# Second FFN of a decoder layer: plain weight units dealt out among mixed ones, a fifth bank, another way for the last gated tile, operand sums sooner

## The chip, the cores and the metric

The kernel runs on one core of a Trainium2 chip. The metric is the device time of one execution in microseconds; lower is better. Engines: TensorE (PE: matmuls, PEld: its weight loads), VectorE (DVE), ScalarE (ACT), GpSimd (POOL) and SyncE (SP). The last two issue most of the transfers here.

## What is computed

One decoder layer on 16 meta tokens and 256 tokens of width 2048, in float32: a half-step gated FFN, an attention and convolution mixer, and a second half-step gated FFN. The change lies in the second FFN:

```python
def swiglu(x, w_gate, w_up, w_down):
    return (jax.nn.silu(x @ w_gate) * (x @ w_up)) @ w_down
...
        u = rms_norm(h, ffn2_norm_g[l])
        h = h + 0.5 * swiglu(u, ffn2_w_gate[l], ffn2_w_up[l], ffn2_w_down[l])
    return h[:, N_META:]
```

Here `h` has 256 rows that count (two tiles of 128 tokens, j = 1 and 2), the weights are 2048 x 5632 (gate, up) and 5632 x 2048 (down).

## The kernel before

**Precision.** Every float32 operand is split into a rounded part and a remainder (`hi`, `lo`; `whi` and `wlo` for weights). A product is three matmuls: hi x hi, hi x lo and lo x hi (`trio`, L467). ScalarE makes `whi` (L237), VectorE makes `wlo = raw - whi` (L238).

**Stages of the second FFN** (`ffn_tokens`, from L730). Tokens are stationary, 512 weight columns stream. The 5632 hidden columns come in 11 tiles of 512, in two groups of 6 and 5 (`GROUPS`). An *up part* computes gate and up of one tile for both token tiles; its gated product goes to `mid`. After a group's up parts come two *down parts* (d = 0 and 2), each for 1024 output columns, which multiply the group's `mid` by the down weights. So the order is: six up parts, two down parts, five up parts, two down parts.

**Mixed blocks.** The sum over k is cut into *quads*: two k blocks of 128 rows, two token tiles and two column halves, that is eight block products. A *plain* quad does all eight (blocks `c`). A *mixed* quad does seven products `P1` to `P7` of sums and differences of blocks (Strassen's scheme in Winograd's form); the weight sums are made early in the kernel by jobs and lie in device memory (`sums_up`, `sums_down`), the operand sums of tokens are made on chip (`combos`). In an up part quads 0 to 4 of 8 are mixed (not in the first part), in a down part quads 0 to 3 of 12 or 10.

**Units.** A *unit* is two weight blocks, 128 x 1024 in all, split by one `whi` and one `wlo` instruction. A plain unit has four products (12 matmuls), a mixed unit two (6 matmuls). `mixed_first` and `plain_first` (L97, L114) list the units of a part; `parts_of_ffn2` joins them. An up part before is: P1 and P2 of all mixed quads, P6, P7, P5 (15 mixed units with P4 and P3 begun), then P3, P4 and the three plain quads, 24 units. A down part begins with plain units.

**Loads.** `loads_of` joins two units of one kind (`h`: straight from the weights, `m`: made sums) into a load of 1 MB if they lie at most four units apart. A load goes to one of four buffers in turn (three `raw`, one `raws`), on SP's queue, in order; a buffer is free when both units in it are split. ScalarE and VectorE run up to four units ahead of TensorE: `whi` and `wlo` have four buffers.

**Order of side work.** `Stream.next` is called once per unit, at = n: it issues the work that is due *first* (even slots of `put`), then the split of unit n + 3, then the work that is *waiting* (odd slots). A slot s means unit s // 2, counted from the moment of the call. `LAG` holds the slots. All engines run their queues in order.

**After an up part** the banks are gathered (`gather`), `silu` runs on ScalarE, `times` on VectorE. Then the gated tile must be turned (tokens to columns). For all tiles but a group's last: two 32 x 32 block turns (`turn_gated`, L717), then `move_blocks`: one write to device memory (`hold`, L725) and four reads back (L728) on POOL's queue, then `split_blocks` (L911, L912). For a group's last tile: sixteen turns of 32 rows each that need no move (`turn_columns`, L590), then `split_last` (L541, L542). Down parts need the last tile where they come to the highest quads: unit 12 of 30 in group 0's first part, unit 8 of 26 in group 1's.

**Banks.** `banks` deals four single banks and two double ones to the sums of a part. In an up part the last quarter of the output, `c[2, 1]`, shares its bank with P1, P5 and P6; `gather` takes both. `copy` (L866) moves a finished sum from a bank to `u`.

Of the kernel before, what the change touches and what calls it, by code (L numbers as in the profile page):

```python
# [15 lines left out]
P = 128  # L16
# [63 lines left out]
    silu=(1, 1), times=(3,), last_turn=(9, 9, 11, 13), last_split=14, drain=(0, 2, 4), below=7,  # L80
    act_combos=(6, 10, 14, 18, 23), act_split=(9, 13, 17, 21, 25), factors=(7, 10, 12), out=(1, 1, 5, 17),
# [15 lines left out]
def mixed_first(mixed, plain):  # L97

    own = in_twos(of_kind("P1", mixed) + of_kind("P2", mixed))
    made = in_twos(sum((of_kind(x, mixed) for x in ("P6", "P7", "P5", "P4")), []))  # L100
    rest = in_twos(of_kind("P3", mixed) + sum(plain_pairs(plain), []))
    early = -(-3 * len(mixed) // 2)
    seq = [("h", x) for x in own] + [("m", x) for x in made[:early]]
    made = made[early:]
    for i, x in enumerate(rest):
        seq.append(("h", x))
        if i >= 2 and i % 2 == 0 and made:
            seq.append(("m", made.pop(0)))
    assert not made
    return seq  # L110


def plain_first(mixed, plain, lead):

    pairs = plain_pairs(plain)
    seq = [("h", x) for x in pairs[:lead]]
    pairs = pairs[lead:]
    seq += [("h", x) for x in in_twos(of_kind("P1", mixed) + of_kind("P2", mixed))]
    for name in ("P6", "P7", "P5", "P4"):
        seq += [("m", x) for x in in_twos(of_kind(name, mixed))]  # L120
        if name in ("P6", "P7"):
            seq.append(("h", pairs.pop(0)))
    seq += [("h", x) for x in in_twos(of_kind("P3", mixed))]
    return seq + [("h", x) for x in pairs]


def parts_of_ffn2():

    out = []
    for g, n in enumerate(GROUPS):  # L130
        for f in range(n):
            mixed = MIXED if g or f else ()
            plain = [i for i in range(8) if i not in mixed]
            seq = mixed_first(mixed, plain) if mixed else [("h", x) for x in plain_pairs(plain)]
            out.append((("up", g, f), mixed, seq))
        for d in (0, 2):
            m = DOWN_MIXED[g][d // 2]
            mixed = tuple(range(m))
            plain = range(m, 2 * n)
            left = 2 * len(plain)  # L140
            out.append((("down", g, d), mixed, plain_first(mixed, plain, left - 2 if not d else left - 8)))
# [156 lines left out]
def tile_decoder_layer(  # L298
# [74 lines left out]
    act = const.tile([P, KD, 2, PITCH], F32R, name="act")  # L373
# [1369 lines left out]
```

## Time and profile before

| what | value |
|---|---|
| median of 3 runs | 2138.37 us (2136.25 to 2138.52) |
| the profiled execution, its own time | 2135.43 us |
| its span, first to last instruction | 2133.3 us |
| mean granted clock of TensorE | 0.997 |
| VectorE, ScalarE busy | 1584.8 us, 1087.0 us |
| first and last matmul of the second FFN (L470) | 1421.6 us, 2127.5 us |

A row of the groups names line, engine, operation, what it writes and reads, shape and count; after the first bar stand the busy time in us and the mean duration of one in ns, after the second the engine's idle time just before such instructions and what ended it. A row of the timeline has start and duration in us, and in brackets the idle time before it and its releaser. A matmul's shown duration overlaps the next one's; the pace is read from the starts.

### The profile page before, as it was taken

The numbers are of one execution on the slowest core, as the hardware profiler recorded it, in microseconds if no ns is written. First come the engines' busy times: TensorE is split into PE (matmuls) and PEld (weight loads), VectorE is DVE, ScalarE is ACT, GpSimd is POOL, SyncE is SP. The second block draws the span as 40 slices with busy tenths as digits, with TensorE's granted clock in tenths as the row PEclk, the third lists the DMA queues.
The fourth block names the chain that finished last, engine by engine and source line by source line (L and its number), as shares of the span: only waits on it lengthen the run. The fifth ranks groups of instructions, "written<-read, shape, count | busy, mean of one in ns | idle before, by whom it ended". The sixth has DMA issues, their size and how long they took to land.

```text
span 2133.3 us, 31823 instructions
## 1 busy us (share of the span) xinstructions
PE 2111.1 (99%) x12704; PEld 1884.9 (88%) x12704; DVE 1584.8 (74%) x2134; ACT 1087.0 (51%) x1373; POOL 128.7 (6%) x225
## 2 busy tenths in 40 slices
PE   9999999999999999999999999999999999999988
PEld 9999999999999998799988888887777788787767
DVE  7667666676676758877688688768787787787786
ACT  6444433344444445465544444457666566666654
POOL 0000000000000000000000000010000000000000
PEclk9999999999999999999999999999999999999999
DMA  7788888889888868855468886677889677889855
GB/s 265 266 319 314 331 313 325 316 316 332 312 325 318 314 216 300 334 181 176 158 245 327 315 316 227 212 261 243 313 316 327 245 276 261 314 306 327 295 210 213
DMA packets 97669, 601.61 MB, mean 282 GB/s; under 512 B 10480, under 2 KB 11248, under 8 KB 36336
## 3 DMA queue, kind: packets, MB, share of 16 engines
q1 hardware_dynamic: 64800, 445.42, 57.4%
q0 software_dynamic: 32144, 153.10, 19.7%
q8 instruction: 99, 1.62, 0.3%
q10 hardware_dynamic: 576, 1.05, 0.2%
q14 instruction: 50, 0.41, 0.1%
HBM read 521.41 MB, written 78.12 MB: 281 GB/s over the span
## 4 chain that ended last, share of the span: by engine, by line
PE 74%; issue 18%; DMA 4%; DVE 2%; ACT 1%; POOL 1%; DVEq 0%; ACTq 0%; POOLq 0%
PE single L470 5%; PE pd L435 4%; PE pd L437 4%; PE pd L436 4%; PE pg L437 4%; PE pu L437 4%; PE pg L436 4%; PE pu L436 4%; PE pu L435 4%; PE pg L435 4%; PE double L470 3%; DMA hold<-mt 3%; PE pgt L463 3%; PE pgt L465 3%; PE pgt L464 3%
## 5 line engine op out<-in xcount | busy, mean ns | idle before, releaser
L238 DVE TENSOR_TENSOR wlo<-raw,whi 128x1024 fp32r<-128x1024 f32 (+1 forms) x762 | 916.1, 1212 | 470.8 <-ACT whi L237 464.3
L237 ACT ACTIVATE whi<-raw 128x1024 fp32r<-128x1024 f32 (+1 forms) x762 | 792.2, 1049 | 849.3 <-PE pd L436 144.4
L435 PE MATMUL pd<-mid,whi 128*128 128x272 f32 x704 | 201.7, 286 | 0.0
L436 PE MATMUL pd<-mid,whi 128*128 128x272 f32 x704 | 201.7, 286 | 0.0
L437 PE MATMUL pd<-mid,wlo 128*128 128x272 f32 x704 | 201.7, 286 | 0.0
L470 PE MATMUL single<-whi,act 128*128 128x512 f32 x552 | 195.0, 390 | 2.0 <-ACT act L794 1.5
L435 PE MATMUL pu<-act,whi 128*128 128x272 f32 x672 | 192.6, 287 | 0.0
L436 PE MATMUL pu<-act,whi 128*128 128x272 f32 x672 | 192.5, 287 | 0.0
L435 PE MATMUL pg<-act,whi 128*128 128x272 f32 x672 | 192.5, 286 | 0.0
L436 PE MATMUL pg<-act,whi 128*128 128x272 f32 x672 | 192.5, 286 | 0.0
L437 PE MATMUL pg<-act,wlo 128*128 128x272 f32 x672 | 192.5, 286 | 0.0
L437 PE MATMUL pu<-act,wlo 128*128 128x272 f32 x672 | 192.5, 286 | 0.0
L645 DVE TENSOR_TENSOR made<-made 128x512 f32<-128x512 f32 x264 | 180.6, 684 | 2.7 <-DMA made<-in_wj_dram 2.7
L470 PE MATMUL double<-whi,act 128*128 128x512 f32 x504 | 180.4, 390 | 0.0
L238 DVE TENSOR_TENSOR wlo<-raws,whi 128x1024 fp32r<-128x1024 f32 (+1 forms) x91 | 108.6, 1207 | 33.8 <-ACT whi L237 33.0
L435 PEld LDWEIGHTS pd<-mid,whi 128*128 128x128 f32 x704 | 132.6, 188 | 0.0
L436 PEld LDWEIGHTS pd<-mid,whi 128*128 128x128 f32 x704 | 132.6, 188 | 0.0
L437 PEld LDWEIGHTS pd<-mid,wlo 128*128 128x128 f32 x704 | 132.6, 188 | 0.0
L437 PEld LDWEIGHTS pu<-act,wlo 128*128 128x128 f32 x672 | 126.6, 188 | 0.0
L435 PEld LDWEIGHTS pu<-act,whi 128*128 128x128 f32 x672 | 126.6, 188 | 0.0
L436 PEld LDWEIGHTS pg<-act,whi 128*128 128x128 f32 x672 | 126.6, 188 | 0.0
L435 PEld LDWEIGHTS pg<-act,whi 128*128 128x128 f32 x672 | 126.6, 188 | 0.0
(342 smaller groups left out, 4353.5 us busy)
## 6 DMA issues: line engine op xcount, KB each, us to landing
raw<-in_wgu_dram SPq DMA_DIRECT2D x86, 1024.0 KB, 6.0
raw<-in_w_dram SPq DMA_DIRECT2D x83, 1024.0 KB, 6.7
made<-in_wj_dram POOLq DMA_DIRECT2D x66, 1024.0 KB, 9.0
sums_up<-made POOLq DMA_DIRECT2D x50, 1024.0 KB, 5.6
raw<-in_wd_dram SPq DMA_DIRECT2D x44, 1024.0 KB, 6.2
raw<-sums_up SPq DMA_DIRECT2D x37, 1024.0 KB, 7.1
raws<-in_w_dram SPq DMA_DIRECT2D x25, 1024.0 KB, 7.0
raw<-in_wcv_dram SPq DMA_DIRECT2D x24, 1024.0 KB, 4.8
```

Source lines behind the costliest of these rows:

```text
L237: nc.scalar.activation(hi[:, :n], raw, AF.Copy)
L238: nc.vector.tensor_sub(lo[:, :n], raw, hi[:, :n].bitcast(F32))
L435: nc.tensor.matmul(ps, whi, xhi, start=first, stop=False)
L436: nc.tensor.matmul(ps, whi, xlo, start=False, stop=False)
L437: nc.tensor.matmul(ps, wlo, xhi, start=False, stop=last)
L463: nc.tensor.matmul(ps, xhi, whi, start=k + i == 0, stop=False)
L464: nc.tensor.matmul(ps, xhi, wlo, start=False, stop=False)
L465: nc.tensor.matmul(ps, xlo, whi, start=False, stop=k + i == n - 1)
L470: nc.tensor.matmul(ps, x(a), w[b], start=first and i == 0, stop=last and i == 2, skip_group_check=halting)
L645: getattr(nc.vector, f"tensor_{op}")(to, a, b)
```

## The change

1. **Up parts** (`mixed_up` for `mixed_first`): the plain units, which stood at the end, are dealt out one after every two mixed units from unit 8 on. The order of kinds is half of P1 and P2, then P7 and P6, and so on. The 24 units are now: eight mixed; then plain ones at 8, 10, 13, 16, 19 and 23 among the mixed.
2. **Fifth bank**: the last quarter `c[2, 1]` has a bank of its own, apart from the one of P1, P5 and P6; so VectorE adds the copy of P5 to that of P7 (one 128 x 512 addition a part more).
3. **Slots**: the three steps of `gather` come at units 0, 2 and 4 of the next part, the second `silu` a unit later, `times` at unit 5, the turns behind the third and fourth plain unit (13, 16).
4. **A group's last gated tile** takes the same way as the others: two turns, one write to device memory, four reads back. It is turned at units 6 and 7 of the down part, moved from unit 8 on, and rounded at units 14 and 15 (group 0) or 10 and 11 (group 1).
5. **First down parts** (`mixed_down`): the plain units that need that tile come after P1 and P2, at unit 16 (group 0) and unit 12 (group 1).
6. **Operand sums** for the down parts are made at units 2, 4, 6, 8 in place of 7, 9, 11, 13, in the same buffers for both groups. The gated tile gets a buffer of its own; `act` is laid out anew, with no instruction more.
7. The blocks of a weight job stand in another order in memory, with the same four sums.

Matmuls, loads by bytes, and splits are the same in number. Lines of the changed kernel lie 4 to 7 further down.

```diff
 LAG = dict(
-    silu=(1, 1), times=(3,), last_turn=(9, 9, 11, 13), last_split=14, drain=(0, 2, 4), below=7,
+    gather=(0, 2, 4), silu=(1, 3), times=10, drain=(0, 2, 4), below=(2, 4, 6, 8, 10),
...
+    half = -(-len(mixed) // 2)
     own = in_twos(of_kind("P1", mixed) + of_kind("P2", mixed))
...
+    made = in_twos(sum((of_kind(x, mixed) for x in ("P7", "P6", "P5", "P4")), []))
     pairs = plain_pairs(plain)
...
+    seq = [("h", x) for x in own[:half]] + [("m", x) for x in made[:half]]
+    rest = [("h", own[half])] + [("m", x) for x in made[half : len(mixed)]] + [None]
...
+    for x in rest:
+        if len(pairs) > 1 and (run == 2 or x is None):
             seq.append(("h", pairs.pop(0)))
...
+def mixed_down(mixed, first, then, last):
...
+    seq = [("h", x) for x in first + own + then[:-2]]
+    for name, more in (("P7", then[-2:-1]), ("P6", then[-1:]), ("P5", []), ("P4", [])):
+        seq += [("m", x) for x in in_twos(of_kind(name, mixed))] + [("h", x) for x in more]
+    return seq + [("h", x) for x in in_twos(of_kind("P3", mixed)) + last]
...
+            if not d:
+                seq = mixed_down(mixed, range(m, 2 * n - 2), range(2 * n - 2, 2 * n), ())
...
-            def banks(apart):
-                one, two = (i for i in range(4) if i not in busy)
-                m = singles[busy[0]] if apart else singles[two]
+            def banks(at_once):
+                free = [i for i in range(4) if i not in held]
+                one, two, m = (*free, held[0]) if at_once else (free[1], held[0], free[0])
...
+            def middle_of(g, f, box, at, then):
+                to = mid[:, 4 * f : 4 * f + 4]
+                put(turn_gated(box), (2 * at[0] + 1, 2 * at[1] + 1))
+                st.put(lambda: move_blocks(box["x"]), 2 * at[1] + 2)
...
-                        put([lambda r=r: turn(r) for r in range(4)], LAG["last_turn"])
-                        st.put(lambda to=to, box=box, f=f, g=g: split_last(to, box["m"], f, g), LAG["last_split"])
+                        middle_of(g, f, box, (6, 7), (4 * n - 10, 4 * n - 9))
```

Two places in the engines' queues. First SP, the loads of the third up part of group 0; `in_w` are blocks straight from the weights, `sums_up_2` made sums; two rows of one buffer name are two of its turns. Before (units 0 and 1, 2 and 3, 4, 5 and 6, 7 and 8, 9 to 12, 13 and 14, 15 and 17, 16 and 19):

```order
L214 DMA raws<-in_w_dram 128x2048
L214 DMA raw<-in_w_dram 128x2048
L214 DMA raw<-in_w_dram 128x1024
L214 DMA raw<-sums_up_2_75 128x2048
L214 DMA raws<-sums_up_2_75 128x2048
L214 DMA raw<-sums_up_2_75 128x2048 x2
L214 DMA raw<-in_w_dram 128x2048
L214 DMA raws<-in_w_dram 128x2048
L214 DMA raw<-sums_up_2_75 128x2048
```

Now (units 0 and 1, 2 and 6, 3 to 5 and 7, 8 and 10, 9 and 12, 11 and 13, 14 and 15, 16 and 19):

```order
L218 DMA raw<-in_w_dram 128x2048
L218 DMA raws<-in_w_dram 128x2048
L218 DMA raw<-sums_up_2_75 128x2048 x2
L218 DMA raw<-in_w_dram 128x2048
L218 DMA raws<-sums_up_2_75 128x2048
L218 DMA raw<-in_w_dram 128x2048
L218 DMA raw<-sums_up_2_75 128x2048
L218 DMA raw<-in_w_dram 128x2048
```

Weights and made sums alternate, and a load's two units may lie four apart: `raws` holds units 2 and 6, and its next load, for units 9 and 12, stands behind unit 6's split.

Second VectorE, in the first down part of group 1, around the turns of the last gated tile (`few` held it before, `gated` holds it now; `few` alone is the operand sums). Before:

```order
L912 TENSOR_TENSOR mid<-mt,mid 128x4x128
L238 TENSOR_TENSOR wlo<-raw,whi 128x1024 x2
L590 STREAM_TRANSPOSE mt<-few 32x2x4x32 x8
L238 TENSOR_TENSOR wlo<-raw,whi 128x1024
L590 STREAM_TRANSPOSE mt<-few 32x2x4x32 x4
L238 TENSOR_TENSOR wlo<-raw,whi 128x1024
L590 STREAM_TRANSPOSE mt<-few 32x2x4x32 x4
L542 TENSOR_TENSOR mid<-mt,mid 128x4x256
L778 TENSOR_TENSOR few<-mid 128x512
```

Now:

```order
L902 TENSOR_TENSOR gated<-u,gated 128x1024
L804 TENSOR_TENSOR mid<-few,mid 128x128
L804 TENSOR_TENSOR below<-few,below 128x3x128
L242 TENSOR_TENSOR wlo<-raw,whi 128x1024
L786 TENSOR_TENSOR few<-mid 128x512
L787 TENSOR_TENSOR few<-few 128x128
L788 TENSOR_TENSOR few<-few 128x128
L789 TENSOR_TENSOR few<-few 128x128
L790 TENSOR_TENSOR few<-few 128x128
L242 TENSOR_TENSOR wlo<-raw,whi 128x1024
L724 STREAM_TRANSPOSE mt<-gated 128x4x4x32
```

The sixteen turns are gone and the low half of `mid` no longer follows them at once; two turns come, behind three sets of operand sums that used to come after the tile.

## What the change does to the time: the prediction

> **What bounds the kernel now.** I began with the page: TensorE is never long idle.
>
> ```profile
> PE 2111.1 (99%) x12704; PEld 1884.9 (88%) x12704; DVE 1584.8 (74%) x2134; ACT 1087.0 (51%) x1373; POOL 128.7 (6%) x225
> ```
>
> The edit leaves all matmuls as they are, so it can only win or lose waits of TensorE inside the second FFN. Second view: its stages side by side (window, its length, TensorE busy, granted clock, DMA share, GB/s), which are the five mixed up parts of group 0, its two down parts, the five up parts of group 1, its two down parts.
>
> ```profile
> 1465.10:1676.20 211.10, 206.80 (x887) 1.00 0.88 313
> 1676.20:1741.60 65.40, 63.41 (x278) 1.00 0.69 243
> 1741.60:1804.20 62.60, 62.60 (x278) 1.00 0.74 265
> 1804.20:2011.50 207.30, 204.49 (x886) 1.00 0.86 314
> 2011.50:2075.50 64.00, 58.00 (x230) 0.92 0.63 217
> 2075.50:2127.90 52.40, 52.14 (x229) 1.00 0.58 214
> ```
>
> By the plan these stages hold 885, 276, 276, 885, 228 and 228 matmuls (an up part 5 x 7 + 3 x 8 products of three; the rows add one or two that lap over an edge). The third has no wait: 62.6 / 276 = 0.227 us each. At that pace the others lose 10.4, 2.8, 6.6, 12.3 and 0.7 us, **32.8 us in all**: the most that can be won. So a unit of two mixed blocks (6 matmuls) lasts 1.36 us and a plain unit (12) 2.72 us. Third view, who TensorE waits for:
>
> ```profile
> PE single L470 <- DVE wlo L238: 7.1, 13, 1.7
> PE single L470 <- ACT mid L541: 3.6, 1, 3.6
> PE double L470 <- DVE wlo L238: 2.2, 10, 0.3
> PE single L470 <- ACT act L794: 1.5, 1, 1.5
> ```
>
> Nearly all are waits for VectorE's low half of a weight unit, and one for the last gated tile. Fourth, that last wait in the timeline:
>
> ```profile
> 2033.30 0.39 PE L470 MATMUL double<-whi,mid 128*128 128x512 f32 x1
> 2037.31 0.80 PE L470 MATMUL single<-whi,mid 128*128 128x512 f32 x1 [3.63 <-ACT mid L541]
> ...
> 2043.43 0.62 PE L470 MATMUL single<-wlo,mid 128*128 128x512 f32 x1
> 2043.86 0.43 PE L470 MATMUL single<-whi,mid 128*128 128x512 f32 x1
> 2044.13 0.40 PE L470 MATMUL double<-whi,mid 128*128 128x512 f32 x1
> ```
>
> After it the starts lie 0.43 us apart, not 0.227, and the clock row says why (0.51):
>
> ```profile
> 2037.00:2044.00 7.00, 6.65 (x15) 0.51 0.22 89
> ```
>
> From 2037.31 to 2044.13 there are 16 matmuls, 6.8 us for 3.6: **a wait that long costs 3.2 us more behind it**.
>
> **The change part by part.** Durations (in each row the mean ns stands after the bar, behind the busy us):
>
> ```profile
> L238 DVE TENSOR_TENSOR wlo<-raw,whi 128x1024 fp32r<-128x1024 f32 x275 | 324.8, 1203 | 98.5 <-ACT whi L237 93.6 <-PE single L470 2.9
> L590 DVE STREAM_TRANSPOSE mt<-few 32x256 f32<-32x256 f32 x32 | 13.9, 436 | 0.5
> L717 DVE STREAM_TRANSPOSE mt<-few 128x512 f32<-128x512 f32 x18 | 12.6, 702 | 0.0
> L912 DVE TENSOR_TENSOR mid<-mt,mid 128x512 fp32r<-128x512 f32 x18 | 12.3, 685 | 5.3 <-ACT mid L911 5.3
> L892 DVE TENSOR_TENSOR few<-u,few 128x1024 f32<-128x1024 f32 x10 | 12.2, 1218 | 0.0
> L875 DVE TENSOR_TENSOR few<-double,u 128x1024 f32<-128x1024 f32 x10 | 12.2, 1217 | 0.0
> L876 DVE TENSOR_TENSOR u<-single,u 128x512 f32<-128x512 f32 x10 | 6.8, 679 | 0.0
> L778 DVE TENSOR_TENSOR few<-mid 128x512 f32<-128x512 f32 x8 | 5.5, 683 | 0.0
> L780 DVE TENSOR_TENSOR few<-few 128x128 f32<-128x128 f32 x13 | 3.8, 292 | 0.4
> L796 DVE TENSOR_TENSOR mid<-few,mid 128x128 fp32r<-128x128 f32 x8 | 2.3, 284 | 0.0
> L796 DVE TENSOR_TENSOR below<-few,below 128x384 fp32r<-128x384 f32 x3 | 1.6, 550 | 0.0
> L237 ACT ACTIVATE whi<-raw 128x1024 fp32r<-128x1024 f32 (+1 forms) x274 | 280.4, 1043 | 148.0 <-PE single L470 68.2 <-PE double L470 44.2 <-DVE wlo L238 11.7
> L866 ACT ACTIVATE u<-single 128x512 f32<-128x512 f32 x46 | 26.9, 585 | 3.6 <-PE single L470 3.6
> L911 ACT ACTIVATE mid<-mt 128x512 fp32r<-128x512 f32 x18 | 11.1, 617 | 8.8 <-DMA mt<-hold 8.8
> ```
>
> *Up parts.* VectorE needs 1.20 us a unit, TensorE 1.36 in a mixed one: 0.16 us to spare. Before, 15 mixed units follow each other while 1.22 + 2 x 0.68 of gathering and 1.22 of multiplying stand at their head; hence two waits a part. Now the gathering is spread over units 0, 2 and 4, the product comes at unit 5, and from unit 8 on a plain unit brings 1.5 us to spare; those two waits go. What is late next is a load. The block load for units 9 and 12 reuses the buffer of the one for units 2 and 6, so it can't be issued before VectorE has split unit 6: three units ahead, where it used to be six. From the part's start, unit 2 ends at 3 x 1.36 = 4.1; ScalarE then copies P1 (0.59) and rounds unit 6 (1.04), VectorE subtracts (1.20): 7.0, with issue times 7.2. Loads that find the queue empty land in (microseconds to landing, min/median/max):
>
> ```profile
> DMA to landing us min/median/max: 4.8/4.8/5.0
> ```
>
> So it lands at 12.0, and 1.04 + 1.20 later, 14.3, unit 9's low half is ready. TensorE wants it 0.23 after 8 x 1.36 + 2.72 = 13.6, at 13.8: 0.5 us late, with the matmul's tail and slower restart 0.8. Ten parts: 8 us. They lose 17.0 now, but not all in waits: of the third view's 9.3 us for low halves, 1.7 is one wait of a down part, and the other 22, most of them here, each cost 0.16 of tail (0.39 - 0.23) and some 0.1 of restart on top. That makes 11.6 or so; the rest is a slower pace, which may stay. The gain lies between 11.6 - 8 = 3.6 and 17.0 - 8 = 9.0; I take the middle, **6.5**. The fifth bank frees no wait that the view shows; its addition (0.68 at unit 18) hides behind plain units. The swapped blocks of the jobs change no count: nothing.
>
> *Last gated tile, group 1.* Sixteen 32-row turns (16 x 0.436 = 7.0) become two (1.4), but a write to device memory and four reads back follow on POOL's queue. VectorE's list from the part's start to the second turn: 8 splits 9.6, gathering 2.6, two low halves 1.4, three sets of operand sums, now ahead of it (0.683 + 4 x 0.29, then 0.83 to split: 2.7 each) 8.0, product 1.2, turns 1.4: 24.2. Neighbours overlap a little and some wait for ScalarE; I take 24. Then the trip. One in the plain part of group 0, and the slowest, with their landings:
>
> ```profile
> 1428.92 0.56 POOL L725 DMA_DIRECT2D hold<-mt  x1 [16.41 <-DVE mt L717]
> 1433.04 2.18 POOL L728 DMA_DIRECT2D mt<-hold  x4 [3.56 <-DMA hold<-mt]
> DMA to landing us min/median/max: 3.8/5.6/5.9
> ```
>
> ```profile
> 2000.76 0.56 POOL L725 DMA_DIRECT2D hold<-mt  x1 [31.01 <-DVE mt L717]
> 2010.74 2.18 POOL L728 DMA_DIRECT2D mt<-hold  x4 [9.43 <-DMA hold<-mt]
> DMA to landing us min/median/max: 7.2/8.3/9.5
> ```
>
> The last of four reads is issued 1.6 after the first: 1433.04 + 1.6 + 5.9 - 1428.92 = 11.7 us, and 20.0 for the other. Here eight plain units run just before and use 0.5 MB in 2.72 us, little more than half the rate of mixed ones, so I take 11.7. The tile is rounded at 24 + 0.3 + 11.7 + 0.6 = 36.6. TensorE wants it at unit 12: 8 x 2.72 + 4 x 1.36 = 27.2. **Wait 9.4 us**, then 3.2 at the low clock, and 0.7 for tails and full VectorE in units 9 to 11: 13.3, against 12.3 now (the 3.63 us wait, its 3.2, and waits for operand sums such as the 1.5 of the third view, which move into plain units and no longer show). **Loss 1.0.** ScalarE waits for the trip at unit 10, with units 13 on queued behind it and VectorE behind those, so nothing else fills the gap.
> On the clock the Trainium skill (TensorE: Matmul & The Clock Gate, What's actually happening) states a window of about 3.4 us: shorter gaps keep full rate, a longer one brings half rate for about one window. By that the restart costs 1.7 us (an estimate), and the sum would be 1.5 lower; the quoted 6.8 us at half rate are twice that, and decide.
>
> *Last gated tile, group 0.* Same list, but it is wanted at unit 16: 12 x 2.72 + 4 x 1.36 = 38.1, and is there at 36.6. The 2.8 us of waits go; I keep 0.8. **Gain 2.0.** The second down parts have nothing to win.
>
> *Sum:* 6.5 + 2.0 - 1.0 = 7.5 us. The profiled execution took 2135.43 us (span 2133.3); it becomes 2127.9. The median of the runs, 2138.37, lies 2.94 above it: **2130.9**. The ends: up gain 3.6 or 9.0; a trip of 10 or 13.5; the low clock at 1.7 or 3.2; group 0 clean or not: 2124 to 2137.
>
> **Rivals.** A measurement here tells 0.2%, 4.3 us, from no change: 2134.1 and 2142.6 are the bounds.
> (1) *The trip stays long, the other side.* All trips of up parts but this one were made beside loads, and the second last tile's own trip keeps ScalarE from its units. At 18 us, group 1 loses 6.3 more, and group 0's tile comes at 42.9 for 38.1: 4.8 + 3.2 - 0.8 = 7.2. That gives 2130.9 + 13.5 = 2144. It turns slower than before from some 15 us. For: nine of ten trips began in busy stretches, with landings such as 9.5. Against: plain units go before. 0.18.
> [...]
> (2) *The late load is later.* If unit 9's load finds another ahead of it, it takes as long as the second of two:
>
> ```profile
> DMA to landing us min/median/max: 5.0/5.8/6.7
> ```
>
> 6.7 for 4.8 is 1.9 us in each of ten parts: 2150. Against: by then the load before it has been out for 8 us. 0.10.
> (3) *The trip is short and the loads in time.* Trip 10, no wait at unit 9: 8 + 1.7 + 1 more: 2120. 0.12.
>
> **How the numbers follow.** Forecast 0.55, rivals 0.18, 0.10, 0.12, rest 0.05. Of the forecast's own range 0.47 lies under 2134.1. Faster 0.47 + 0.12 + 0.02 = 0.61; same 0.18; slower 0.21. The range, 2121 to 2146, takes in rival 1, and leaves out rival 2 and the ends.
>
> **What would show it.** Right: no wait at units 3 and 5 of an up part, one of 0.3 to 0.6 us at unit 9 for the low half, its release by a DMA; one wait of 8 to 11 us at unit 12 of group 1's first down part, a clock near 0.5 behind it; none in group 0's. Wrong: two waits a part as before; a trip over 15 or under 9 us; a wait at unit 16 in group 0.

## The result and the profile after

| | before | changed |
|---|---|---|
| median | 2137.62 us (2136.25 to 2138.52) | 2164.80 us (2163.59 to 2165.60) |
| the profiled execution, its own time and span | 2135.43, 2133.3 us | 2164.98, 2163.2 us |
| mean granted clock | 0.997 | 0.990 |

The ratio is 1.0127 (95% interval 1.011 to 1.0145): slower by 27 us, where 7.5 us of gain were forecast. Four runs of each. Lines of the changed kernel (4 to 10 further down than before): `whi` L241, `wlo` L242, matmuls L477, the copies of banks L876, the tile's split L921 and L922, its trip L732 and L735.

The stages of the changed kernel, as in the prediction's second view (five mixed up parts of group 0, its two down parts, five up parts of group 1, its two down parts):

```profile
1465.25:1683.65 218.40, 208.41 (x886) 168.82 (x885) 170.02 (x161) 142.48 (x159) 12.24 (x23) 0.98 0.81 299
1683.65:1754.15 70.50, 65.81 (x277) 52.11 (x276) 50.88 (x72) 39.27 (x50) 4.20 (x8) 0.98 0.70 246
1754.15:1816.75 62.60, 62.60 (x278) 51.83 (x277) 47.21 (x47) 33.58 (x34) 0.00 (x0) 1.00 0.73 272
1816.75:2034.75 218.00, 209.41 (x887) 170.32 (x886) 169.69 (x159) 139.87 (x154) 10.12 (x19) 0.97 0.83 296
2034.75:2105.30 70.55, 56.45 (x230) 44.23 (x229) 46.21 (x68) 35.24 (x46) 3.58 (x7) 0.90 0.64 212
2105.30:2157.70 52.40, 52.13 (x229) 42.52 (x227) 39.97 (x43) 26.02 (x27) 2.20 (x4) 1.00 0.56 215
```

After the window stand its length, then busy time and count of TensorE, its weight loads, VectorE, ScalarE and GpSimd, then the granted clock, the DMA share and GB/s. Length less 0.2268 us for each matmul (885, 276, 276, 885, 228, 228) is what a stage loses: 17.7, 7.9, 0.0, 17.3, 18.8 and 0.7, in all 62.3 us (the starts of the matmuls, unrounded). Before they lost 32.7. The difference, 29.6, is the whole of the span's 29.9, and it lies in three places: the up parts 17.0 to 34.9, group 0's first down part 2.8 to 7.9, group 1's 12.3 to 18.8. Who TensorE waits for there (in all, times, the longest):

```profile
PE double L477 <- ACT u L876: 18.4, 10, 2.7
PE single L477 <- ACT mid L921: 10.6, 2, 8.4
PE single L477 <- DVE wlo L242: 4.7, 6, 1.0
PE double L477 <- DVE wlo L242: 2.5, 2, 1.7
PE single L477 <- ACT whi L241: 1.1, 2, 0.7
```

The first row did not exist before: one wait in each mixed up part for ScalarE's copy of a bank. The timeline of the second mixed up part, units 5 and 6:

```profile
1514.73 0.40 PE L477 MATMUL double<-whi,rs_y 128*128 128x512 f32 x1
1514.73 1.22 DVE L242 TENSOR_TENSOR wlo<-raw,whi 128x1024 fp32r<-128x1024 f32 x1
...
1515.42 0.40 PE L477 MATMUL single<-whi,act 128*128 128x512 f32 x1
1515.87 1.22 DVE L902 TENSOR_TENSOR gated<-u,gated 128x1024 f32<-128x1024 f32 x1
...
1517.18 0.60 ACT L876 ACTIVATE u<-double 128x512 f32<-128x512 f32 x1 [1.38 <-DVE gated L902]
...
1517.83 0.50 PE L477 MATMUL double<-whi,act 128*128 128x512 f32 x1 [2.01 <-ACT u L876]
```

Read from the end: the matmul at 1517.83 is P2's (unit 6). It waits 2.01 us for the copy of P7's sum, which is ScalarE's at 1517.18; that one waits 1.38 us for VectorE's `times` (L902), since the copy overwrites the `u` that `times` still reads; and `times`, due at unit 5, stands behind a weight split. P2 needs no result of any of these. It writes `c[1, 0]`, P7's sum lies in `c[2, 0]`: two banks, but the two halves of one double tile.

In seven of the ten parts the matmuls behind this wait run at half clock, so in the next part (starts 0.43 us apart):

```profile
1560.42 0.50 PE L477 MATMUL double<-whi,act 128*128 128x512 f32 x1 [2.01 <-ACT u L876]
...
1562.23 0.63 PE L477 MATMUL single<-whi,act 128*128 128x512 f32 x1
1562.65 0.63 PE L477 MATMUL single<-wlo,act 128*128 128x512 f32 x1
1563.08 0.63 PE L477 MATMUL single<-whi,act 128*128 128x512 f32 x1
```

Three stretches of 3.41 us there, the first with the wait in it; the granted clock is 0.50 in the second alone:

```profile
1558.14:1561.55 3.41, 1.40 (x7) 0.95 (x6) 2.76 (x3) 1.65 (x2) 0.00 (x0) 1.00 0.91 312
1561.55:1564.96 3.41, 3.41 (x10) 2.63 (x9) 1.26 (x2) 2.35 (x3) 0.00 (x0) 0.50 1.02 425
1564.96:1568.38 3.42, 3.42 (x17) 2.78 (x16) 2.67 (x3) 1.79 (x3) 0.00 (x0) 1.00 0.84 285
```

So such a part loses 2.2 us at the wait (starts 2.4 apart for 0.23) and 1.6 by eight slow matmuls: 3.8 of the 4.1 us that most up parts lose now.

The down parts: ScalarE's waits for a tile's trip, four in all, two in each group's first down part (before, 8.8 us in two):

```profile
L921 ACT ACTIVATE mid<-mt 128x512 fp32r<-128x512 f32 x22 | 13.6, 619 | 29.1 <-DMA mt<-hold 29.1
```

Group 0's second-last tile is one of the four: the part began at 1683.65, and ScalarE stood 7.64 us from unit 1 on, with the splits of units 4 and up queued behind. First the rows of before, where the part began at 1676.18 and ScalarE stood 4.11 us, then those of now:

```profile
1665.42 0.56 POOL L725 DMA_DIRECT2D hold<-mt  x1 [31.01 <-DVE mt L717]
...
1684.91 0.63 ACT L911 ACTIVATE mid<-mt 128x512 fp32r<-128x512 f32 x1 [4.11 <-DMA mt<-hold]
```

```profile
1672.83 0.56 POOL L732 DMA_DIRECT2D hold<-mt  x1 [31.86 <-DVE mt L724]
...
1682.93 2.18 POOL L735 DMA_DIRECT2D mt<-hold  x4 [9.54 <-ACT whi L241]
...
1693.48 0.63 ACT L921 ACTIVATE mid<-mt 128x512 fp32r<-128x512 f32 x1 [7.64 <-DMA mt<-hold]
```

And the last tile of group 1, the one the prediction was about:

```profile
2065.57 0.56 POOL L732 DMA_DIRECT2D hold<-mt  x1 [29.03 <-DVE mt L724]
...
2069.50 2.18 POOL L735 DMA_DIRECT2D mt<-hold  x4 [3.37 <-DMA hold<-mt]
...
2077.26 0.63 ACT L921 ACTIVATE mid<-mt 128x512 fp32r<-128x512 f32 x1 [9.08 <-DMA mt<-hold]
...
2077.95 0.80 PE L477 MATMUL single<-whi,mid 128*128 128x512 f32 x1 [8.43 <-ACT mid L921]
```

From the write's issue to ScalarE's start are 2077.26 - 2065.57 = 11.7 us; TensorE waits 8.43. All its waits in this part:

```profile
PE single L477 <- ACT mid L921: 8.4, 1, 8.4
PE single L477 <- DVE wlo L242: 2.5, 3, 1.0
PE double L477 <- DVE wlo L242: 2.5, 2, 1.7
PE single L477 <- ACT whi L241: 0.7, 1, 0.7
```

By the starts of the matmuls, the 18.8 us that this part loses are 3.5 at units 4 and 5 (behind ScalarE's stand), 3.9 at units 9 to 11 (low halves), 8.6 at the tile and 2.8 in slow matmuls behind it. Group 0's 7.9 are 3.3 at units 4 and 5, 2.3 at the last tile (unit 16) and 2.3 in slow matmuls behind it.

### The profile page after: what moved, and what is told of

It is laid out like the page before. It is cut to its first block, busy times and chain, and to the rows that moved or that the text cites. A ratio compares the mean times of both kernels' runs of the same rounds, so it can differ in the third digit from the quotient of the medians.

```text
span 2163.2 us, 31827 instructions
## 1 busy us (share of the span) xinstructions
PE 2118.0 (98%) x12704; PEld 1893.2 (88%) x12704; DVE 1587.6 (73%) x2120; ACT 1090.2 (50%) x1377; POOL 134.2 (6%) x235
## 4 chain that ended last, share of the span: by engine, by line
PE 77%; issue 14%; DMA 4%; DVE 3%; ACT 1%; POOL 1%; SPq 0%; DVEq 0%; POOLq 0%; ACTq 0%
PE single L477 7%; PE double L477 6%; PE pd L443 4%; PE pd L442 4%; PE pd L444 4%; PE pu L442 4%; PE pg L442 4%; PE pg L444 4%; PE pu L444 4%; PE pu L443 4%; PE pg L443 4%; PE pgt L472 3%; PE pgt L470 3%; PE pgt L471 3%; DMA hold<-mt 2%
## 5 line engine op out<-in xcount | busy, mean ns | idle before, releaser
L242 DVE TENSOR_TENSOR wlo<-raw,whi 128x1024 fp32r<-128x1024 f32 (+1 forms) x763 | 924.7, 1215 | 467.3 <-ACT whi L241 457.6
L241 ACT ACTIVATE whi<-raw 128x1024 fp32r<-128x1024 f32 (+1 forms) x763 | 798.5, 1051 | 850.7 <-PE pd L443 146.2
L477 PE MATMUL double<-whi,act 128*128 128x512 f32 x544 | 201.6, 398 | 18.4 <-ACT u L876 18.4
L477 PE MATMUL single<-whi,act 128*128 128x512 f32 x584 | 216.3, 395 | 0.0
L477 PEld LDWEIGHTS double<-whi,act 128*128 128x128 f32 x544 | 103.5, 190 | 44.3 <-ACT u L876 22.7
L242 DVE TENSOR_TENSOR wlo<-raws,whi 128x1024 fp32r<-128x1024 f32 (+1 forms) x90 | 106.9, 1191 | 43.5 <-ACT whi L241 41.9
L477 PEld LDWEIGHTS single<-whi,act 128*128 128x128 f32 x584 | 112.1, 192 | 24.3
L444 PEld LDWEIGHTS pg<-act,wlo 128*128 128x128 f32 x672 | 126.6, 188 | 0.0
```

The lines of the kernel that those rows point to most:

```text
L241: nc.scalar.activation(hi[:, :n], raw, AF.Copy)
L242: nc.vector.tensor_sub(lo[:, :n], raw, hi[:, :n].bitcast(F32))
L444: nc.tensor.matmul(ps, wlo, xhi, start=False, stop=last)
L477: nc.tensor.matmul(ps, x(a), w[b], start=first and i == 0, stop=last and i == 2, skip_group_check=halting)
```

## The experiments

What a stage loses in each kernel, worked out as above (one profiled execution each; ratios to before with their 95% intervals from all runs of the kernel; before, measured beside them, had a median of 2134.6 to 2134.9 us):

| kernel | ten up parts | group 0 first down | group 1 first down | all | ratio |
|---|---|---|---|---|---|
| before | 17.0 | 2.8 | 12.3 | 32.7 | 1 |
| changed | 34.9 | 7.9 | 18.8 | 62.3 | 1.0127 (1.011, 1.0145) |
| 1 times sooner | 30.1 | 8.9 | 16.1 | 55.7 | 1.0094 (1.0076, 1.0113) |
| 2 P7 in another bank | 13.0 | 7.8 | 16.7 | 38.1 | 1.0029 (1.0019, 1.004) |
| 3 P2 ahead of P7 | 15.3 | 7.8 | 15.7 | 39.4 | 1.0055 (1.0038, 1.0072) |
| 4 not dealt out | 14.2 | 1.0 | 16.3 | 32.1 | 1.0011 (1.0001, 1.002) |
| 5 own bank for P7 | 9.0 | 9.9 | 17.6 | 37.2 | 1.0014 (1.0004, 1.0023) |
| 6 kernel 3, tile turned sooner | 18.6 | 1.4 | 11.6 | 32.3 | 1.000 (0.999, 1.0009) |
| 7 kernel 3, sums later | 16.7 | 1.4 | 13.0 | 31.8 | 1.0006 (0.9989, 1.0023) |
| 8 kernel 3, last tile used later | 20.2 | 8.0 | 10.5 | 38.8 | 1.001 (0.9999, 1.0021) |
| 9 kernel 5, tile turned sooner | 9.4 | 0.0 | 10.0 | 20.0 | 0.9945 (0.9932, 0.9957) |
| 10 kernel 9, sums later | 9.2 | 1.5 | 10.3 | 21.6 | 0.9949 (0.9936, 0.9961) |
| 11 kernel 10, old turn | 8.7 | 5.4 | 9.5 | 24.2 | 0.9964 (0.995, 0.9978) |
| 12 kernel 9, last tile used later | 9.7 | 0.0 | 3.2 | 13.0 | 0.9911 (0.9897, 0.9925) |

The up parts of one order differ between single executions by some microseconds (kernels 3, 6, 7 and 8 have the same up parts but for two turns: 15.3 to 20.2), so the two or three microseconds there are not read. The profiled executions of kernels 1 and 8 took 4.6 and 7.1 us more than the kernel's median, that of kernel 3 took 4.1 less; the sums in the table are of these executions, the ratios of all runs.

### 1 to 4: the wait in the up parts

**1.** `times` two units sooner:

```diff
-    gather=(0, 2, 4), silu=(1, 3), times=10,
+    gather=(0, 2, 4), silu=(1, 3), times=6,
```

> The changed kernel with one number changed: in the second FFN's up parts the product of gate and up value (VectorE, the times step) falls due at unit 3 of the next part and not at unit 5. In the changed kernel's trace ScalarE's copy of product seven's bank (512.. 0.6 us long) starts 2.05 us after that bank's last matmul, because it overwrites what times still reads, and times stands behind a weight split on VectorE. Theory A (TensorE's 2.0 us wait at unit 6 is this copy's lateness, and 8 matmuls at half clock follow it): the copy then waits only for ScalarE's split in hand, the wait falls to 0.5 to 0.8 us, no half clock follows, each of the 9 affected up parts loses about 1.0 to 1.5 us instead of 4.1: 25 to 28 us less, 2137 to 2141 us. Rival B (the copy is late because ScalarE and VectorE are behind with the splits as a whole, times being only what they happen to do then): the wait comes back as a wait for whi or wlo at units 6 to 9, under 8 us less, 2157 to 2165 us. In both the two down parts stay as they are (7.9 and 18.8 us lost).

Measured: 2154.76 us, 7 us less (by the ratios). That is a miss for A; it is within B's "under 8 us less", but the wait did not become one for a split, as B had it. The wait was still there, 14.7 us in all, with another cause in front of the copy. Its timeline in the fourth mixed part:

```profile
1601.24 1.22 DVE L902 TENSOR_TENSOR gated<-u,gated 128x1024 f32<-128x1024 f32 x1
...
1603.13 1.06 ACT L241 ACTIVATE whi<-raw 128x1024 fp32r<-128x1024 f32 x1 [1.03 <-DMA raw<-in_w_dram]
...
1604.10 0.58 ACT L876 ACTIVATE u<-double 128x512 f32<-128x512 f32 x1
...
1604.73 0.50 PE L477 MATMUL double<-whi,act 128*128 128x512 f32 x1 [1.93 <-ACT u L876]
```

`times` is done by 1602.46, but the copy stands on ScalarE behind a split that waits 1.03 us for a load. That split is for a unit TensorE wants later; alone it would hold nobody up. So `times` was one of two things that make the copy late; what makes its lateness cost is that TensorE asks for it.

**2.** P7 in a bank that no matmul touches before unit 8, order unchanged:

```diff
-                        copies = dict(P1=copy(1, m), P6=copy(2, m), P7=copy(3, c[2, 0]), P5=fifth)
+                        copies = dict(P1=copy(1, m), P6=copy(2, m), P7=copy(3, c[2, 1]), P5=fifth)
...
-                    quads(c, m, c[2, 0], act_part, act_of, mixed, seq, copies)
+                    quads(c, m, c[2, 1], act_part, act_of, mixed, seq, copies)
```

> The changed kernel with product seven of the up parts put into the single bank of the second half's second quarter, which no matmul touches again before unit 8, and copied from there; all instructions and their order stay. The output is another sum of the same products (product seven is missing in one bank and is too many in another), the work is the same. Theory A1 (there is no use of data behind the wait: product two's bank and product seven's bank are the two halves of one double tile, and TensorE's write into the first waits for ScalarE's read of the second): the wait at unit 6 goes altogether, times stays late and costs nothing since the bank is wanted again only at unit 8, 3.6 us later: 28 to 31 us less, 2134 to 2137 us. Rival A2 (the copy itself is what TensorE needs, through the operand u or the bank order): no change or a wait of 1 us or more at unit 8, 2150 to 2165 us. Rival B (engines behind as a whole): 2157 to 2165 us.

Measured: 2141.75 us, some 21 us less, where A1 had 28 to 31. No wait for a copy is left among TensorE's. The up parts fall from 34.9 to 13.0. The copy is as late as before, and nobody wants it. The three longest of TensorE's waits; the third is new and stands in the first mixed part alone, where P7 (unit 5) now goes to a bank that `times` of the plain part still reads:

```profile
PE single L477 <- ACT mid L921: 9.7, 2, 7.1
PE single L477 <- DVE wlo L242: 7.7, 11, 1.0
PE single L477 <- DVE gated L903: 3.3, 1, 3.3
```

**3.** P1 and P2 complete ahead of P7, plain units still dealt out:

```diff
-    seq = [("h", x) for x in own[:half]] + [("m", x) for x in made[:half]]
-    rest = [("h", own[half])] + [("m", x) for x in made[half : len(mixed)]] + [None]
-    rest += [("h", x) for x in own[half + 1 :]] + [("m", x) for x in made[len(mixed) :]]
+    seq = [("h", x) for x in own] + [("m", x) for x in made[:half]]
+    rest = [("m", x) for x in made[half : len(mixed)]] + [None]
+    rest += [("m", x) for x in made[len(mixed) :]]
...
```

The steps of the gated tile keep the unit numbers that they have in the changed kernel.

> The changed kernel with the up parts' units in another order: all of products one and two first, as before the change, then product seven, six, five and four with the plain units dealt out among them (10, 13, 16, 19, 22, 23); the steps of the gated tile stay at the units at which they were. Theory A: product two no longer follows product seven's copy in the shared double tile; the first write to that tile after product seven is a plain unit two units later; the wait goes and with it the half clock: up parts lose 5 to 12 us in all instead of 35, 2135 to 2143 us. Rival B (the dealing out itself overloads ScalarE or the loads at units 4 to 10): the waits only change place, 2155 to 2165 us.

Measured: 2146.12 us median (the profiled run 2142.07); up parts 15.3. The wait for the copy is gone, as A had it. The time is 3 us above A's range, and so are the up parts (5 to 12): waits for `wlo` grew from 4.7 and 2.5 us in the changed kernel to 10.1 and 5.2. The down parts keep their 24.

**4.** The order of before (`mixed_first`), all else kept, the unit numbers of the gated tile's steps too. The weight jobs keep their new order, so products six and seven take each other's sums.

```diff
-            seq = mixed_up(mixed, plain) if mixed else [("h", x) for x in plain_pairs(plain)]
+            seq = mixed_first(mixed, plain) if mixed else [("h", x) for x in plain_pairs(plain)]
...
```

> The changed kernel with the up parts' unit order of before (plain units at the end), while the fifth bank, the early operand sums, the last gated tile's way over device memory and the down parts' order stay. Theory A says that the up parts' loss is the order's alone: they go back to about 17 us lost (10.4 and 6.6 before) from 35, the down parts keep their 27: 2146 to 2149 us, so some 10 us slower than before, all of it in the first down part of each group. Rival C (the fifth bank, the late gather or the early sums cost as much as the order): the up parts stay above 25 us lost, 2155 us or more. The prediction's own reading (dealing out gains 6.5 us in the up parts once its waits are cured) would put this kernel 6 us above the third of these runs.

Measured: 2137.44 us, 9 us better than A's range. The up parts came to 14.2 (17 expected; before 17.0), and group 0's first down part to 1.0 where 7.9 was expected. The second has its reason in the trace: with the plain units at the end, units 13 and 16 come sooner in microseconds, so the second-last tile's trip started 29.1 us after its part's start and not 33.4, and ScalarE stood 1.1 us for it and not 7.6. In group 1 the trip started at 29.7 us but took 20.8 us and not 16.6; ScalarE stood 5.4 us, and the part lost 16.3.

### 5 to 8: a repair of the banks, and the down parts

**5.** The change's own order, with the banks dealt out so that P7 has one to itself:

```diff
-                c = {(1, 0): x[:, 0], (2, 0): x[:, 1], (1, 1): singles[one], (2, 1): singles[two]}
+                c = {(1, 0): x[:, 0], (1, 1): x[:, 1], (2, 0): singles[one], (2, 1): singles[two]}
...
-                    lambda: add(s, x, u[:, 1:3]),
+                    lambda: [add(s[:, j - 1], c[j, 0], u[:, j]) for j in (1, 2)],
...
```

> The changed kernel, unit order and all, with the banks dealt out so that product seven has a bank to itself: the double tile now holds the two quarters of the first half, and the second half's two quarters lie in single banks (the gather adds the first quarter in two pieces). Theory A1 (a false wait by the shared double tile, shown by the second run at 21 us): TensorE's next write to product seven's bank is unit 8, so the wait at unit 6 and the half clock behind it go: up parts 11 to 16 us lost in all, down parts as in the changed kernel (25 to 27): 2138 to 2144 us. Rival F (what the second run saved came of the product missing in a bank, or the banks held by the last part now wait at unit 0 instead): 2148 us or more.

Measured: 2137.51 us, some 24 us less than the changed kernel, with the same instructions but for gathers in two pieces; a little better than the range, as are the up parts with 9.0. Group 1's up parts (the second row) have no wait at all now; after the window stand its length and TensorE's busy time:

```profile
1465.71:1674.60 208.89, 204.56 (x887) 165.16 (x886) 168.15 (x165) 141.45 (x159) 11.81 (x22) 1.00 0.85 312
...
1809.65:2011.30 201.65, 201.65 (x887) 166.13 (x886) 167.70 (x163) 138.68 (x154) 10.23 (x19) 1.00 0.89 320
```

**6.** Kernel 3 with the second-last tile turned at units 11 and 12:

```diff
-                        middle_of(g, f, box, at[2:4], [length + i for i in then])
+                        middle_of(g, f, box, (11, 12) if f == n - 2 else at[2:4], [length + i for i in then])
```

> The third run (products one and two first; 2146 us, up parts 15.3, first down parts 7.8 and 15.7 us lost) with one more edit: the second-last gated tile of each group is turned at units 11 and 12 of the next part and not at 13 and 16, so that its trip over device memory starts four units (6 to 8 us) sooner. Theory D (the first down part's added loss is ScalarE standing 7.4 us at that tile's split, until the 17 to 20 us trip lands, with TensorE starved at units 4 and 5 for it): ScalarE's wait falls to 1 us or less, group 0's first down part loses 1 to 3 us, group 1's 12 to 14 (the last tile's own wait stays): 8 to 10 us less, 2135 to 2138 us. Rival E (the trip is bound by the loads it shares the queues with, and takes as much longer as it starts sooner): ScalarE's wait stays above 5 us and the time within 2 us of the third run.

Measured: 2133.51 us, as D said, and 1.5 us better than its range. ScalarE's wait for trips goes from 27.6 us (kernel 3, first row) to 10.4 (second), which is the last tiles' alone:

```profile
L921 ACT ACTIVATE mid<-mt 128x512 fp32r<-128x512 f32 x22 | 13.6, 619 | 27.6 <-DMA mt<-hold 27.6
```

```profile
L921 ACT ACTIVATE mid<-mt 128x512 fp32r<-128x512 f32 x22 | 13.6, 617 | 10.4 <-DMA mt<-hold 10.4
```

The trip did not get longer for starting sooner (18.2 and 16.5 us from issue to the last landing; 21.9 and 21.9 in kernel 3), so E falls.

**7.** Kernel 3 with the operand sums where they had been:

```diff
-    below=(2, 4, 6, 8, 10),
+    below=(7, 9, 11, 13, 15),
```

> The third run with the operand sums of the down parts put back to units 7, 9, 11, 13 (the change has them at 2, 4, 6, 8). Theory G (the sums, now ahead of and among the last gated tile's turns on VectorE, put off its second turn and so its trip): in group 1 the second turn, now 29.4 us after the part's start, comes 2 to 4 us sooner, TensorE's wait for the last tile falls by as much, and the part loses 12 to 13.5 us instead of 15.7; group 0 within 1 us: 2 to 4 us less than the third run. Rival H (the second turn waits for ScalarE's standing still behind the second-last tile, which holds VectorE's splits too, and the sums fill VectorE's idle time for nothing): within 1 us of the third run, or slower by up to 3 us because the sums now stand in the way of the mixed units' splits.

Measured: 2134.83 us (2129.84 to 2148.97), a wide spread, so the time decides nothing. The profile has group 0's second-last trip 4 us shorter (18.0 for 21.9 us); no run shows the sums to do that, and 6.4 of the gain lie there. In group 1, where the trip took 21.2 for 21.9 us and ScalarE still stood 6.9, the second turn is 6 us sooner, more than G said, and the waits for `wlo` at units 9 to 11 are gone. TensorE comes to unit 12 sooner too (28.4 us after the part's start for 34.2), so the wait there stays (7.5 for 7.0), and the part loses 13.0, as G had it. While ScalarE stands still, the early sums do put off the turn. Kernel 10 has them later where it does not.

**8.** Kernel 3 with group 1's first down part in another order:

```diff
+    if len(first) != 8:
...
+    seq = [("h", x) for x in first + own]
+    for name, more in (("P7", []), ("P6", []), ("P5", []), ("P4", then[:2])):
+        seq += [("m", x) for x in in_twos(of_kind(name, mixed))] + [("h", x) for x in more]
+    three = in_twos(of_kind("P3", mixed))
+    return seq + [("h", x) for x in three[:1] + then[2:3] + three[1:] + then[3:] + last]
...
-                        middle_of(g, f, box, (6, 7), (4 * n - 10, 4 * n - 9))
+                        middle_of(g, f, box, (6, 7), (19, 19) if g else (4 * n - 10, 4 * n - 9))
```

> The third run with another order of group 1's first down part: products seven, six, five and four come straight behind one and two, and the four plain units that read the last gated tile stand among product three at the end, so that the tile is needed at unit 20, 38 us of matmuls after the part's start, and not at unit 12 (27 us); its split on ScalarE falls due at unit 19. Theory I (the chain turn, trip, split ends about 37 to 41 us after the part's start, so the wait is a matter of where the first use stands): the wait of 7.1 to 8.4 us and the 3 us at half clock behind it go; the part loses 4 to 7 us instead of 15.7: 8 to 11 us less than the third run, 2135 to 2138 us. Rival J (twelve mixed units in a row ask more of VectorE than its 1.2 us split in each 1.36 us leaves, with turns, sums and tile splits beside them): 4 to 8 us come back as waits for wlo, under 4 us less, 2142 us or more.

Measured: 2135.48 us, within I's range. The part loses 10.5 for 15.7: the long wait is gone (0.6 us for ScalarE, 0.6 for VectorE at the tile's first uses). The waits for `wlo` that are left, up to 1.7 us, are not J's: all but one of 0.3 us stand before unit 12, at units 4, 5 and 9 to 11, as in kernel 3, ahead of the mixed units that the edit moved. Of the 10.5 us, 5.9 are lost there.

### 9 to 12: together

**9.** Kernel 5 with the edit of kernel 6.

> The fifth run (the change's own unit order, product seven in a bank of its own; 2137.5 us, up parts 9.0, first down parts 9.9 and 17.6 us lost) with the second-last gated tile turned at units 11 and 12 instead of 13 and 16. Theory: two independent losses stood in the change, the shared double tile (some 25 us) and the second-last tile's trip (6 to 8 us in group 0, 4 to 6 in group 1), and the rest of the change gains about 8 us in the up parts: ScalarE's stands of 9.9 and 8.4 us go, the first down parts lose 1 to 2 and 11.5 to 13.5 us, the whole 2123 to 2127 us, 8 to 12 us faster than before. Rival (the up parts' gain and the sooner turn take from each other: the turn now falls on the plain units' places, and VectorE or the queues push it back into the splits): 2130 us or more.

Measured: 2123.04 us, at the lower end of the theory. Both first down parts:

```profile
1673.80:1736.35 62.55, 62.55 (x277) 51.80 (x276) 51.75 (x73) 39.96 (x50) 2.74 (x5) 1.00 0.78 280
...
2001.45:2063.10 61.65, 53.52 (x229) 43.72 (x228) 46.64 (x69) 36.01 (x46) 2.74 (x5) 0.94 0.69 245
```

Group 0's has no wait left, group 1's one for the last tile (the first row here; the second row's five lie in up parts):

```profile
PE double L477 <- ACT mid L921: 8.1, 1, 8.1
PE single L477 <- DVE wlo L242: 3.1, 5, 0.8
```

**10.** Kernel 9 with the edit of kernel 7.

> The kernel of the run before it in this call with the down parts' operand sums at units 7, 9, 11, 13 instead of 2, 4, 6, 8. Theory G (the early sums stand ahead of the last tile's second turn on VectorE): the last tile's second turn comes 1 to 3 us sooner and group 1's first down part loses 1 to 3 us less: 1 to 3 us less in all. Rival H (with ScalarE no longer standing still the early sums fill idle time): within 1 us, or up to 3 us slower since the sums then stand before the mixed units' splits.

Measured: 2123.50 us, the same. The last tile's second turn starts 22.1 us after its part's start in both kernels. H: where ScalarE doesn't stand still, the place of the sums costs nothing that the times show.

**11.** Kernel 10 with the last gated tile turned by 16 transposes again:

```diff
-                        middle_of(g, f, box, (6, 7), (4 * n - 10, 4 * n - 9))
...
+                        put([lambda r=r: turn(r) for r in range(4)], (11, 11, 13, 15))
+                        st.put(lambda to=mid[:, 4 * f : 4 * f + 4], box=box, f=f, g=g: split_last(to, box["m"], f, g), 16)
```

> The kernel of the run before it in this call (sums later) with each group's last gated tile turned as before the change, by 16 transposes on VectorE (7.0 us by the trace of before, 1.4 for the two of the change) and split at once at unit 8, with no trip over device memory. Theory K (the trip of 11.6 us and the queue position of its split are what makes group 1's first down part wait 7.5 to 8.4 us and run 3 us at half clock; 5.6 us more of VectorE in that stage cost less): the wait for the last tile goes or falls under 3 us, 2 to 5 us come back as waits for wlo, the part loses 4 to 8 us instead of 11 to 13: 4 to 9 us less. Rival L (VectorE is as late without the trip, as before the change, where this part lost 12.3 us with the same 16 transposes): the part loses 11 us or more, no gain or up to 4 us slower.

Measured: 2127.09 us, 3.6 us slower than kernel 10, in time as L had it, though the part's loss lies between K and L: no wait for the tile itself is left, but group 1's part loses 9.5 us (10.3 with the trip) and group 0's 5.4 (1.5), mostly in waits for weight splits:

```profile
PE double L477 <- DVE wlo L242: 5.9, 8, 1.2
PE double L477 <- ACT whi L241: 3.0, 1, 3.0
PE single L477 <- DVE wlo L242: 2.9, 5, 0.8
```

ScalarE stands 7.1 us at the tile's split here too, for VectorE's last transpose. The way over device memory is the better one by 4 us in group 0 and a tie in group 1.

**12.** Kernel 9 with the order of kernel 8.

> The first kernel of this call with group 1's first down part in the order of the eighth run (products seven, six, five, four ahead of the four plain units that read the last gated tile, its split at unit 19). In the eighth run the wait for the tile fell to 0.6 and 0.6 us, but 4 us of waits for wlo came in the run of mixed units and the part lost 10.5 us, of which 3 us stood at its first units for the second-last tile. Theory I: without that stand the part loses 5 to 8 us: 4 to 7 us less than the first kernel of this call. Rival J (the waits for wlo grow, since twelve mixed units in a row are bound by VectorE): the part loses 10 us or more, within 2 us of the first kernel of this call.

Measured: 2115.81 us, the best: 0.9911 of before, 7 us less than kernel 9, as much as theory I had at most. ScalarE waits for no trip any more, and the part loses 3.2 us. Its row of ScalarE's splits, and its window:

```profile
L927 ACT ACTIVATE mid<-mt 128x512 fp32r<-128x512 f32 x22 | 13.5, 616 | 0.0
```

```profile
2001.50:2056.45 54.95, 52.95 (x229) 42.40 (x228) 50.82 (x75) 35.35 (x46) 2.74 (x5) 1.00 0.80 290
```

VectorE is busy 50.82 of 54.95 us, so J's bound is near. But the 5.9 us that kernel 8 lost before unit 12 are gone with ScalarE's stand at the second-last tile; the 4 us of waits for `wlo` that the expectation puts into the run of mixed units stood there.

## Why the prediction was wrong

**What bounds it: right.** The pace stayed 0.2268 us (the third stage has it in both traces), and the whole difference is TensorE's waits in the named stages.

**Up parts: wrong, the step that failed.** The text said "Now the gathering is spread over units 0, 2 and 4, the product comes at unit 5 ... What is late next is a load", and counted the fifth bank and the order of kinds at nothing. It followed weights and VectorE from unit to unit, but not the banks: who reads a bank that TensorE writes next. The new order puts P7 between the two halves of P2; P7's sum and P2's share a double tile; so TensorE now asks for ScalarE's copy at once, and the copy was made late by that very edit, `times` at unit 5. Before, P2 was complete when P7 began, and the copy was never asked for. Kernel 2 (no instruction added, moved or removed) and kernel 5 show it: 34.9 us lost fall to 13.0 and 9.0. Kernel 1 shows that curing one reason for the late copy is not enough.

With that wait away, the forecast's own term comes out near: kernel 5's up parts lose 9.0 for 17.0, a gain of 8.0 where 6.5 (3.6 to 9.0) was worked out. (The lower end took the waits of before in the up parts as 11.6 us; by the starts of the matmuls they were 19 waits and 9.8.) Part of that is luck, since the late load at unit 9 was to cost 0.8 us in each of ten parts and is half a hit: kernel 9's waits at the place where it was put are 0.3 to 0.8 us in group 0's five parts, none in group 1's. In the changed kernel itself there was none at that place: ScalarE waited 1.9 to 3.8 us for that load in group 0's parts there too, but TensorE came later, by its wait at unit 6.

**The low clock: right in kind, short of one case.** The text priced it for a wait of 3.6 us only. Here waits of 2.0 to 2.7 us drew it too, seven of eight, which is 7 x 1.6 = 11 us of the loss. The rule of the Trainium skill that the prediction weighed (TensorE: Matmul & The Clock Gate, What's actually happening) has shorter gaps than 3.4 us at full rate; the trace disagrees from 2.0 us on (kernel 1's from 1.9). The trace of before had a case already, which the prediction passed over: behind waits of 1.48 and 0.52 us that end at 2055.94 and 2057.18, the granted clock is 0.50 from 2057.57 to 2060.98.

**Last tile, group 1: the trip right, the rest late on both sides.** The trip took 11.7 us as worked out (issue to ScalarE's start). But the second turn, put at 24 us after the part's start, was done at 30.5, and TensorE came to unit 12 at 34.6 us and not at 27.2. Both were late behind ScalarE's stand at the second-last tile, so it is luck that their difference, the wait, came to 8.4 for 9.4. The slow matmuls behind it cost 2.8 for 3.2. The loss was 18.8 for 13.3 because of what came before unit 12: 7.4 us, where the sum had 0.7. The operand sums, which the sum only added to VectorE's list, have a share in that: in kernel 7 they come later, and with ScalarE standing 6.9 us the waits at units 9 to 11 are gone and the turn is done at 24.1. In kernel 9 there is no stand: the turn is done at 22.8, TensorE is at unit 12 at 27.2 and waits 8.1, and the part loses 10.0, with 1.7 for the 3.2 at the low clock. There the steps hold.

**Last tile, group 0: wrong by what stands before it.** "Gain 2.0" became a loss of 5.1. ScalarE's stand costs 3.3 us at units 4 and 5, and it put off the last tile too: the tile was to be there at 36.6 us, ScalarE came to split it at 43.0, and TensorE waited 2.2 us, with slow matmuls behind. In kernel 9 that stand is gone and the part loses nothing: the full gain of 2.8.

**Rival 1 named the mechanism and priced another.** It said the second-last tile's trip "keeps ScalarE from its units", but worked out a longer last trip. The last trips were short (12.3 and 11.6 us to the last landing). The second-last ones took what they took before (20.6 and 20.9 us; 19.5 and 20.0 before), but ended 9.8 us into group 0's part and not 8.7, and ScalarE came to the split at 2.2 us and not at 4.6, because it is now due at unit 1 and not 2: so 7.6 us of standing for 4.1. The change sets that unit in the line `then = (1, 2)`, and no term of the sum had it. Kernels 6 and 9 show what a sooner trip is worth: 11.7 and 14.7 us by the ratios, what the stand cost before included. A later unit for that split was not tried by itself. Rivals 2 and 3 did not happen.

Kernel 9 is the change without the two waits that the sum did not have; its second-last tile is turned sooner than the change has it. It gains 11.5 us (2134.59 to 2123.04) where 7.5 were forecast: by stages 7.6 for 6.5 in the up parts, 2.8 for 2.0 in group 0's first down part, and a gain of 2.3 for a loss of 1.0 in group 1's. The two waits cost 24 us (the changed kernel to kernel 5) and some 15 (kernel 5 to 9).

## What to carry to other kernels

When units change places, write down for every bank who reads it last and who writes to its tile next, not only which weights are ready: a wait that stood for nothing comes alive when a writer moves behind a reader. Two banks in one tile counted as one for such a wait here. And for a step that is due on an in-order engine at a unit, compare the time at which the engine gets there with the landing of what it reads; everything queued behind pays the difference.

## What the runs showed of the hardware

The granted clock falls after gaps shorter than expected: seven of the eight waits of 2.0 us or more in the up parts were followed by some 3.4 us of matmuls 0.43 us apart, beginning up to 1.4 us after the restart, and the two waits of 1.1 and 0.2 us were not. By the granted clock the seven slow stretches last 3.413 us each and start 44.37 us or 218.45 us apart, which is 13 and 64 times 3.413; around the 8.4 us wait the clock is 0.50 for 13.65 us, four times 3.413. The stretches of kernel 1's trace lie on such a grid too (the first two start at 1605.76 and 1650.13). That fits a window of that length that runs on by itself, as the Trainium skill has it (the same page and section), with the addition that a window in which TensorE stood most of the time is enough. The one 2.0 us wait without a slow stretch (1515.8 to 1517.8) lies across an edge of that grid (1517.18); the seven lie within a window each. That is read from traces and not tried by itself.

The Trainium skill (Perfetto Trace Analysis, Matmuls) advises to let independent groups of matmuls rotate through banks, so that the evacuation of one overlaps the next. Here the banks were different ones and the evacuation still did not overlap, until they were different tiles too (kernels 2 and 5).
